# Block products for seven of u's eight column pairs, with sums made by GpSimd, and v's items ahead of them

## The chip, the cores and the metric

One core of one Trainium2 chip runs the whole kernel. The metric is the device time in microseconds of one execution; a measured time is the median over several runs. The profile shows one execution. Its engines are PE (TensorE: matmuls), PEld (TensorE's weight loads, which overlap PE), DVE (VectorE), ACT (ScalarE), POOL (GpSimd) and SP (SyncE, which here only starts DMA transfers). A profile's span runs from its first instruction to its last.

## The reference, cut to what matters

One decoder layer on x of 1024 tokens by 1024 channels, in float32. The change touches the input projection, and in it the columns of u:

```python
h = rms_norm(x, attn_norm_w[l])
proj = h @ w_in[l]
q, k, v, u, g = jnp.split(proj, splits, axis=-1)
...
u_a, u_b = jnp.split(u, 2, axis=-1)
c = causal_depthwise_conv(u_a * jax.nn.sigmoid(u_b), conv_w[l], conv_b[l])
c = jax.nn.silu(layer_norm(c, conv_ln_w[l], conv_ln_b[l]))
y_b = c @ w_proj_conv[l]
```

u has 2048 columns. Column c of its first half is multiplied with the sigmoid of column c of its second half, so the kernel works on eight column pairs: 128 columns of `u_a` and the same 128 of `u_b`. The convolution has 31 taps along the tokens and works on each channel by itself.

## The kernel before

**Numbers in two parts.** A float32 matrix is held as a high part (rounded to the matmul's type, by `split_hi` on ScalarE, line 120) and a low part (the rest, source less high part, by `split_lo` on VectorE, line 125, or by GpSimd in `wsplit`, line 284, while `low_by_pool` is set). A product of two matrices is three matmuls per block: high by high, high by low, low by high (`mm3`, lines 162 to 164).

**The first stage**, from the start to about 320 us. `opening` normalizes x, turns it and writes h transposed as `hT_hi` and `hT_lo` (128 partitions x 8 blocks of the contraction x 1024 tokens), beside v's first 256 columns and the first half of u's pair 0. Then come items in a list: `first`, which is U1, V1, U2, U3, V2, U4, Q0, V3, U5, U6, U7. A `U` item (`u_item`, `u_half`) takes a column pair: for each half of the tokens it makes the gate's product (`gemm_T`, 8 blocks x 3 matmuls of 512 tokens into one PSUM bank), the sigmoid on ScalarE, the other product, their multiplication on VectorE from PSUM (line 601), and a store to `u_d`. A `V` item makes 256 columns of v for all tokens in four yields (`gemm_N`, matmuls of 256 columns), splits them (`v_split`) and stores them; a `Q` item makes one head's q and k in four yields, normalizes them, and turns them with `turn_qk`, whose results are copied between partition halves by SP's DMAs (line 800 on).

**Weights** come through `ws`, a stream of planned loads: a DMA on SP's queue into one of two buffers `wraw`, then the split into `whi` and `wlo` of 1024 columns, of which there are three each. `ws.ahead` says how many loads are made before they are asked for.

**The convolution** is a background list, `bg`. When a pair's u is stored, `conv_load` (its reload) and 31 taps are added: a first tap (line 570, VectorE) and 30 more (line 578, VectorE), each a multiply-add of up to 1023 tokens onto a running sum. The sums of channels 0 to 3 (`CONV_PSUM`) lie in PSUM, one at a time, and are copied out by ScalarE after the last tap (line 582); those of channels 4 to 7 lie in SBUF. After every yield of the first stage `bg.step` issues on average 3.25 entries (`TAPS_FIRST`), behind the last low part made by VectorE. What is left is spread over the attention stage by its slack on VectorE, and must be done at that stage's end.

**The bias rows** (`bias_rows`, at n = 16): GpSimd's queue loads a table of one-hot rows `oh` and the bias table `rb`, TensorE multiplies them in three pieces of 384 columns, ScalarE copies the pieces into `gr`, and one DMA on GpSimd's queue stores all to `b_d`. `bias_skew(h)`, one per head, are further DMAs on GpSimd's queue, at every third yield from n = 18.

**What sets the order.** Each engine runs its instructions in one queue, in an order that is fixed when the kernel is built, by a planner that follows the order in the program and its own estimate of when an instruction is ready; `after(ins)` puts the instructions of a block behind `ins` on its engine. An instruction that waits holds everything behind it on its engine. A buffer of a tag with `bufs=n` is reused after n tiles.

**The gate/up stage** late in the kernel already uses seven products where eight are plain: `prepare(f)` makes the sums of weight quarters, `differences` makes the sums of the activations (`T`), `product` is one block product (4 blocks x 3 matmuls onto one bank), and `pair` runs the seven over three PSUM banks a, b, c. A bank that is used a second or third time keeps on accumulating, and what it holds in between is copied out.

Of the kernel before, what the change touches and what calls it, by code (L numbers as in the profile page):

```python
# [16 lines left out]
P = 128  # L17
# [40 lines left out]
def kernel(  # L58
# [48 lines left out]
    sm.tile([P, 40], F32, name="pad_sm", bufs=1)  # L107
# [19 lines left out]
    low_by_pool = [False]  # L127

# [43 lines left out]
    pg2 = a0.enter_context(tc.tile_pool(name="pg2", bufs=2, space=PSUM))  # L172
# [107 lines left out]
    def wsplit(raw, tiles=wtiles):  # L280
        hi, lo = tiles()
        split_hi(hi[:], raw[:])
        if low_by_pool[0]:
            pool.tensor_tensor(lo[:], raw[:], f32(hi[:]), op=ALU.subtract)
        else:
            split_lo(lo[:], raw[:], hi[:])
        return hi, lo
# [100 lines left out]
    first = ["U1", "V1", "U2", "U3", "V2", "U4", "Q0", "V3", "U5", "U6", "U7"]  # L388
# [11 lines left out]
    TAPS_FIRST = 3.25  # L400
# [11 lines left out]
    for it in ["U0"] + first + [x_ for l_ in later for x_ in l_]:  # L412
        ws.plan(loads_of(it))
# [148 lines left out]
    def conv_taps(c):  # L562
        acc = []

        def first_tap():
            if c < CONV_PSUM:
                acc.append(pcv[0].tile([P, S], F32, tag="acc", name=f"acc{c}", bufs=1))
            else:
                acc.append(cv.tile([P, S], F32, tag="acc", name=f"acc{c}", bufs=1))
            dve.tensor_scalar(  # L570
                acc[0][:], us[c][:], cw[:, c, CW - 1 : CW], pcol("conv_b", c), op0=ALU.mult, op1=ALU.add
            )
# [140 lines left out]

    def v_split(o, j, i2):
        vh = ap.tile([P, 512], F32R, tag="vh", name=nm("vh"))
        vl = ap.tile([P, 512], F32R, tag="vl", name=nm("vl"))
# [17 lines left out]
    def bias_rows():  # L734

        oh = ap.tile([NB + 1, TL], F32, name="oh", bufs=1)
        pool.dma_start(oh[:], buckets)
        rb = ap.tile([NB + 1, H], F32, name="rb", bufs=1)
        pool.memset(rb[:], -BIG)
        pool.dma_start(rb[:NB, :], rel_bias)  # L740
        dve.tensor_scalar(rb[:], rb[:], -1.0, None, op0=ALU.mult)
        gr = ap.tile([H, TL], F32, name="gr", bufs=1)
        for c0 in range(0, TL, 384):
            o = pm()
            pe.matmul(o[:H, :384], rb[:], oh[:, c0 : c0 + 384], start=True, stop=True)
            act.copy(gr[:, c0 : c0 + 384], o[:H, :384])
        pool.dma_start(b_d[:], gr[:])
# [87 lines left out]

    def opening():


        nonlocal qkp
# [131 lines left out]
        pcv.append(pcv_ctx.enter_context(tc.tile_pool(name="pcv", bufs=1, space=PSUM)))  # L971
        low_by_pool[0] = True
# [8 lines left out]
    for _ in chain(opening(), run(first)):  # L981
# [4 lines left out]
        if n >= 18 and n % 3 == 0 and (n - 18) // 3 < H:  # L986
            bias_skew((n - 18) // 3)
# [816 lines left out]
```

## Time and profile before

| what | us |
|---|---|
| median of 3 runs | 1760.24 (1760.22 to 1760.38) |
| the profiled execution | 1758.51 |
| its span | 1756.7 |
| TensorE busy (a model of overlapped matmuls) | 1744.9 |
| VectorE busy | 1251.9 |
| ScalarE busy | 816.9 |
| GpSimd busy | 82.0 |

A row of the costliest groups gives line, engine, operation, written and read tiles with their shapes, the count, then busy us and mean ns of one, then the idle time before them and what ended it. A row of the timeline gives start, duration, engine, line and operation, neighbours of one kind merged with their count; in brackets stands the idle time before it and what ended it. A row of a tile or a line gives the count, the smallest, median and largest duration in ns, and the first and the last start. A row of TensorE's waits gives who waited, for whom, the total in us, the times and the longest. A row of DMA issues ends with the KB of each and the us to landing.

### The profile page before, as it was taken

The numbers are of one execution on the slowest core, as the hardware profiler recorded it, in microseconds if no ns is written. First come the engines' busy times: TensorE is split into PE (matmuls) and PEld (weight loads), VectorE is DVE, ScalarE is ACT, GpSimd is POOL, SyncE is SP. The second block draws the span as 40 slices with busy tenths as digits, with TensorE's granted clock in tenths as the row PEclk, the third lists the DMA queues.
The fourth block names the chain that finished last, engine by engine and source line by source line (L and its number), as shares of the span: only waits on it lengthen the run. The fifth ranks groups of instructions, "written<-read, shape, count | busy, mean of one in ns | idle before, by whom it ended". The sixth has DMA issues, their size and how long they took to land.

```text
span 1756.7 us, 25779 instructions
## 1 busy us (share of the span) xinstructions
PE 1744.9 (99%) x9377; PEld 1503.8 (86%) x9377; DVE 1251.9 (71%) x2084; ACT 816.9 (47%) x1900; POOL 82.0 (5%) x121
## 2 busy tenths in 40 slices
PE   9999999999999999999999999999999999999999
PEld 7888998989998998988788788888888888888887
DVE  7487878798888988977778534877667666565544
ACT  5121341667677777755457313643333333333332
POOL 2113222000000000000000000000000000000000
PEclk9999999999999999999999999999999999999999
DMA  6246363143335344343873544234544544598663
GB/s 208 86 132 210 108 199 102 43 145 102 98 110 151 100 121 127 91 138 121 286 248 106 168 168 144 91 102 151 173 150 160 177 154 140 168 359 286 215 217 131
DMA packets 253156, 271.68 MB, mean 155 GB/s; under 512 B 15666, under 2 KB 177498, under 8 KB 253028
## 3 DMA queue, kind: packets, MB, share of 16 engines
q1 hardware_dynamic: 250848, 263.25, 46.3%
q0 software_dynamic: 1744, 5.19, 1.0%
q8 instruction: 74, 1.21, 0.3%
q10 hardware_dynamic: 436, 1.58, 0.3%
q14 instruction: 54, 0.44, 0.1%
HBM read 175.55 MB, written 78.16 MB: 144 GB/s over the span
## 4 chain that ended last, share of the span: by engine, by line
PE 94%; DVE 3%; DMA 1%; ACT 1%; issue 1%; SPq 0%; DVEq 0%
PE acc L1650 22%; PE pg L164 14%; PE pg L162 14%; PE pg L163 14%; PE acc L494 12%; PE sc L1043 2%; PE sc L1042 2%; PE pT L1081 2%; PE wo L164 2%; PE wo L163 2%; PE wo L162 2%; DVE acc L578 1%; PE pW L162 1%; PE pW L163 1%; PE pW L164 1%; PE pg L863 1%
## 5 line engine op out<-in xcount | busy, mean ns | idle before, releaser
L578 DVE SCALAR_TENSOR_TENSOR acc<-u,cw,acc 128x1023 f32<-128x1023 f32 (+14 forms) x240 | 307.3, 1281 | 3.8
L120 ACT CAST whi<-wraw 128x1024 fp32r<-128x1024 f32 x107 | 112.5, 1053 | 200.7 <-PE pg L163 95.3
L162 PE MATMUL pg<-hT_hi,whi 128*128 128x512 f32 x512 | 201.7, 394 | 0.0
L163 PE MATMUL pg<-hT_lo,whi 128*128 128x512 f32 x512 | 201.0, 393 | 0.0
L164 PE MATMUL pg<-hT_hi,wlo 128*128 128x512 f32 x512 | 200.8, 393 | 0.0
L162 PE MATMUL pg<-whi,hT_hi 128*128 128x256 f32 x704 | 199.6, 284 | 0.0
L164 PE MATMUL pg<-whi,hT_lo 128*128 128x256 f32 x704 | 199.6, 284 | 0.0
L163 PE MATMUL pg<-wlo,hT_hi 128*128 128x256 f32 x704 | 199.4, 283 | 0.0
L125 DVE TENSOR_TENSOR wlo<-draw,whi 128x1024 fp32r<-128x1024 f32 x75 | 91.7, 1223 | 85.8 <-ACT whi L120 77.6
L125 DVE TENSOR_TENSOR wlo<-wraw,whi 128x1024 fp32r<-128x1024 f32 x85 | 103.6, 1219 | 60.3 <-ACT whi L120 60.1
L120 ACT CAST whi<-draw 128x1024 fp32r<-128x1024 f32 x75 | 79.1, 1055 | 129.5 <-PE acc L494 116.0
L163 PEld LDWEIGHTS pg<-wlo,hT_hi 128*128 128x128 f32 x704 | 134.5, 191 | 1.8
L162 PEld LDWEIGHTS pg<-whi,hT_hi 128*128 128x128 f32 x704 | 134.3, 191 | 1.7
L164 PEld LDWEIGHTS pg<-whi,hT_lo 128*128 128x128 f32 x704 | 134.4, 191 | 1.2
L494 PE MATMUL acc<-wlo,whi 128*128 128x512 f32 x308 | 119.8, 389 | 0.0
L494 PE MATMUL acc<-whi,wlo 128*128 128x512 f32 x308 | 119.8, 389 | 0.0
L1049 ACT ACTIVATE E<-E,mn 128x640 f32<-128x640 f32 (+7 forms) x128 | 99.6, 780 | 41.3 <-DVE mn L1044 40.9
L164 PEld LDWEIGHTS pg<-hT_hi,wlo 128*128 128x128 f32 x512 | 96.2, 188 | 19.7 <-issue 0.6
L162 PEld LDWEIGHTS pg<-hT_hi,whi 128*128 128x128 f32 x512 | 96.3, 188 | 18.7 <-issue 0.6
L163 PEld LDWEIGHTS pg<-hT_lo,whi 128*128 128x128 f32 x512 | 96.3, 188 | 18.6
L1044 DVE CUSTOM_DVE_ANT_0 E<-sc,tb 128x512 f32<-128x512 f32 (+3 forms) x128 | 74.0, 585 | 31.2 <-PE pT L1081 16.1
L1650 PE MATMUL acc<-h_hi,whi 128*128 128x512 f32 x240 | 93.4, 389 | 0.0
(299 smaller groups left out, 4097.3 us busy)
## 6 DMA issues: line engine op xcount, KB each, us to landing
wraw<-in_w_gate_up_dram SPq DMA_DIRECT2D x44, 512.0 KB, 4.6
wraw<-in_w_in_dram SPq DMA_DIRECT2D x40, 512.0 KB, 4.0
qs<-qs SPq DMA_DIRECT2D x96, 128.0 KB, 2.3
wd<-in_w_down_dram SPq DMA_DIRECT2D x44, 256.0 KB, 3.2
tdT<-wd SPq DMA_DIRECT2D x88, 128.0 KB, 4.8
draw<-sdS SPq DMA_DIRECT2D x44, 256.0 KB, 3.4
draw<-tdT SPq DMA_DIRECT2D x44, 256.0 KB, 3.6
wraw<-in_w_in_dram SPq DMA_DIRECT2D x32, 256.0 KB, 3.2
```

Source lines behind the costliest of these rows:

```text
L120: act.copy(dst, src)
L125: last_lo[0] = dve.tensor_tensor(dst, src, f32(hi), op=ALU.subtract).ins
L162: pe.matmul(o, lh, rh, start=start, stop=False)
L163: pe.matmul(o, lh, rl, start=False, stop=False)
L164: last_mm[0] = pe.matmul(o, ll, rh, start=False, stop=stop).ins
L494: m = pe.matmul(o[s_][i][:], l_[:, ts], r_[:, 512:], start=start and j + y_ == 0, stop=j == n - 1 and y_ == 2, skip_group_check=not start,)
L578: dve.scalar_tensor_tensor(a_, us[c][:, : S - n], cw[:, c, t : t + 1], a_, op0=ALU.mult, op1=ALU.add)
L1042: pe.matmul(o[:, :w], qh[:, qs], k, start=True, stop=False)
L1043: last_mm[0] = pe.matmul(o[:, :w], ql[:, qs], k, start=False, stop=True).ins
L1044: dve.tensor_tensor_reduce(e[:, ks], o[:, :w], tb[:, S - nk + c0 : S - nk + c0 + w], 1.0, mn[:, j : j + 1] if c0 else 3.0e38, ALU.add, ALU ...
L1049: act.activation(e[:, :nk], e[:, :nk], AF.Exp, bias=mn[:, j : j + 1], scale=-1.0, accum_out=l[:, j : j + 1])
L1650: pe.matmul(o[:], a_[x_][:, k, :], b_[y_][:, k, :], start=start and k + x_ + y_ == 0, stop=k == 3 and x_ == 1, skip_group_check=not start,)
```

## The change

For u's pairs 1 to 7 the eight quarter products (two column blocks x two halves of the contraction x two halves of the tokens) are replaced by seven block products, each of half the contraction and half the tokens, on sums of quarters:

- `sums_of_h` makes the four sums of h's quarters, T1 to T4: GpSimd joins high and low part of each quarter (8 additions of 1024 columns), VectorE makes the differences (8 subtractions of 1024), ScalarE the high parts and GpSimd the low parts (8 of 1024). It is issued in three steps after each of the first four yields.
- `prepare` is moved out of the gate/up stage and takes its source as arguments; while `low_by_pool` is set GpSimd makes its four weight sums (512 columns each) and the low parts. In the gate/up stage it is called as before, through `prep`.
- `u_pair` runs the seven products with four yields a pair, the copies, sigmoids and sums of each output half, one multiplication on GpSimd and one on VectorE, the two stores, and adds the convolution's entries.
- `first_stage` replaces the list: V1, V2, then U1 to U7, then Q0 and V3. The weights of pair 1 are loaded at n = 4 and prepared by n = 7 of its own count.
- The first tap of a channel goes from VectorE to ScalarE; 2.75 background entries are issued for each yield, behind VectorE's last instruction, and after the first stage entries are issued until channels 0 to 3 are complete.
- `bias_rows` works in three calls (n = 18, 19, 20), each with its own load, matmul, copy and store, in buffers of the u stage; the skews come at every second yield from n = 24.
- The tiles of `opening` are released before the u stage, whose rooms `tt` and `st` take their place and that of `qkp`, which is opened after it. PSUM banks of `pg2` stay open to the end of the stage.

```diff
-    first = ["U1", "V1", "U2", "U3", "V2", "U4", "Q0", "V3", "U5", "U6", "U7"]
+    first = ["V1", "V2"]
+    last = ["Q0", "V3"]
...
-            dve.tensor_scalar(
-                acc[0][:], us[c][:], cw[:, c, CW - 1 : CW], pcol("conv_b", c), op0=ALU.mult, op1=ALU.add
-            )
+            act.activation(acc[0][:], us[c][:], AF.Identity, bias=pcol("conv_b", c), scale=cw[:, c, CW - 1 : CW])
...
+    def bias_rows(c0):
+
+        if c0 == 0:
+            pool.memset(rb[:], -BIG)
+            pool.dma_start(rb[:NB, :], rel_bias)
+            dve.tensor_scalar(rb[:], rb[:], -1.0, None, op0=ALU.mult)
+        oh, gr = half("u3")[: NB + 1, :384], half("u2")[:H, :384]
+        pool.dma_start(oh, buckets[:, c0 : c0 + 384])
+        o = pm()
+        pe.matmul(o[:H, :384], rb[:], oh, start=True, stop=True)
+        act.copy(gr, o[:H, :384])
+        pool.dma_start(b_d[:, c0 : c0 + 384], gr)
...
+        def add(j, l):
+            def go():
+                for e in range(2):
+                    ks = slice(4 * j + 2 * e, 4 * j + 2 * e + 2)
+                    pool.tensor_tensor(
+                        F[j, l][:, two[e], :], f32(hT_hi[:, ks, TOK[l]]), f32(hT_lo[:, ks, TOK[l]]), op=ALU.add
+                    )
+
+            return go
+
+        def less(o, a_, b_):
+            def go():
+                for e in two:
+                    dve.tensor_tensor(*[F[x_][:, e, :] for x_ in (o, a_, b_)], op=ALU.subtract)
+
+            return go
...
+        def parts(z, tags, src, eng):
+            def go():
+                hi, lo = [room(t_, F32R, f"T{z}{e}") for t_, e in zip(tags, "hl")]
+                v = src or fourth
+                for e, v_ in zip(two, v):
+                    split_hi(hi[:, e, :], v_)
+                for e, v_ in zip(two, v):
+                    eng.tensor_tensor(lo[:, e, :], v_, f32(hi[:, e, :]), op=ALU.subtract)
+                TS[z] = hi[:], lo[:]
+
+            return go
...
+        return [
+            add(*f11), add(*f12), less(f11, f12, f11), add(*f22), less(f12, f22, f12), less(f22, f22, f11),
+            parts(2, ("y0", "y1"), halves(f22), pool), add(*f21), parts(1, ("y2", "y3"), halves(f11), pool), less4,
+            parts(3, ("x00", "x11"), halves(f12), pool), parts(4, ("x01", "x10"), None, pool),
+        ]
...
+        s12, s34 = [s_pool.tile([P, 1024], F32, tag=t_, name=nm(t_), bufs=1) for t_ in ("s12", "s34")]
+        A["11"], A["12"] = parts(*[t_[:] for t_ in wsplit(raws[0])])
+        eng = pool if low_by_pool[0] else dve
+        eng.tensor_tensor(s12[:, 0:512], a21, a22, op=ALU.add)
+        eng.tensor_tensor(s12[:, 512:1024], s12[:, 0:512], a11, op=ALU.subtract)
+        eng.tensor_tensor(s34[:, 0:512], a11, a21, op=ALU.subtract)
+        eng.tensor_tensor(s34[:, 512:1024], a12, s12[:, 512:1024], op=ALU.subtract)
+        yield A
+        A["S1"], A["S2"] = parts(*[t_[:] for t_ in wsplit(s12)])
+        yield
+        A["S3"], A["S4"] = parts(*[t_[:] for t_ in wsplit(s34)])
+        hi, lo = [s_pool.tile([P, 512], F32R, tag=t_, name=nm(t_), bufs=s_bufs) for t_ in ("sh", "sl")]
+        split_hi(hi[:], a22)
+        low(lo[:], a22, hi[:])
...
+    def u_pair(c, A, ahead):
+
+        B = {(j, l): (hT_hi[:, KH[j], TOK[l]], hT_lo[:, KH[j], TOK[l]]) for j in range(2) for l in range(2)}
+        a, b, c_ = acc(), acc(), acc()
+        product(b, A["11"], B[0, 0], True)
+        p1 = half("p1")
+        act.copy(p1, b[:])
+        product(a, A["12"], B[1, 0], True)
+        dve.tensor_tensor(p1, a[:], p1, op=ALU.add)
+        act.activation(p1, p1, AF.Sigmoid)
+        nxt = next(ahead, None)
+        yield
+        product(b, A["S2"], TS[2], False)
+        u2 = half("u2")
+        act.copy(u2, b[:])
+        product(c_, A["S1"], TS[1], True)
+        u3 = half("u3")
+        act.copy(u3, c_[:])
+        next(ahead, None)
+        yield
+        product(b, A["S3"], TS[3], False)
+        dve.tensor_tensor(u3, b[:], u3, op=ALU.add)
+        product(c_, A["S4"], B[1, 1], False)
+        dve.tensor_tensor(u2, c_[:], u2, op=ALU.add)
+        act.activation(u2, u2, AF.Sigmoid)
+        pool.tensor_tensor(u3, u3, u2, op=ALU.mult)
+        nc.sync.dma_start(u_d[c][:, TOK[1]], u3)
+        yield
+        product(b, A["22"], TS[4], False)
+        dve.tensor_tensor(p1, b[:], p1, op=ALU.mult)
+        nc.sync.dma_start(u_d[c][:, TOK[0]], p1)
+        bg.todo.insert(max(0, len(bg.todo) - CW), conv_load(c))
+        bg.add(conv_taps(c))
+        next(ahead, None)
+        yield
+        return nxt
+
+    def first_stage():
...
+        for n, _ in enumerate(run(first)):
+            for _ in range(3):
+                if tsum:
+                    tsum.pop(0)()
+            if n == 1:
+                ws.ahead = 1
+                ws.fetch()
+                ws.ahead = 0
+            if n == 4:
+                next(ups[0])
+            if n == 5:
+                A = next(ups[0])
+            if n in (6, 7):
+                next(ups[0])
+            yield
+        for c in range(1, NKT):
+            ahead = ups[c] if c < NKT - 1 else weights_ahead()
+            next(ahead)
+            A = yield from u_pair(c, A, ahead)
...
-        if n == 16:
-            with after(last_of(mybir.EngineType.DVE)), after(bias_anchor[0]):
-                bias_rows()
-        if n >= 18 and n % 3 == 0 and (n - 18) // 3 < H:
-            bias_skew((n - 18) // 3)
-        due += TAPS_FIRST
-        with after(last_lo[0]):
+        if n in (18, 19, 20):
+            with after(bias_anchor[0]):
+                bias_rows(384 * (n - 18))
+        if n >= 24 and n % 2 == 0 and (n - 24) // 2 < H:
+            bias_skew((n - 24) // 2)
+        due += 2.75
+        with after(last_of(mybir.EngineType.DVE)):
             bg.step(int(due))
...
+    bg.until((NKT - CONV_PSUM) * (CW + 1) - 1)
     low_by_pool[0] = False
```

More of the change, by code (lines that the diff above doesn't have):

```diff
@@ L282, in wsplit @@
         split_hi(hi[:], raw[:])
[L283 to L286, printed above, removed]
+        low(lo[:], raw[:], hi[:])
         return hi, lo
```

154 lines of the change are left out of this document (89 added, 65 removed).

## The prediction

> **What bounds the kernel now.** I read the totals by engine first, then the longest waits of TensorE, then busy times by stage: 58 to 320 us is the stage of v, u and the first q/k, 320 to 830 attention, 1173 to 1560 the gate/up product, which already works in blocks.
>
> ```profile
> span 1756.7 us, 25779 instructions
> PE 1744.9 (99%) x9377; PEld 1503.8 (86%) x9377; DVE 1251.9 (71%) x2084; ACT 816.9 (47%) x1900; POOL 82.0 (5%) x121
> ...
> PE pg L162 <- DVE gt L1378: 2.9, 1, 2.9
> PE pm L200 <- DVE busy L187: 1.5, 1, 1.5
> ...
> 58.00:96.00 38.00, 38.00 (x200) 32.78 (x199) 22.07 (x20) 6.38 (x8) 7.19 (x3) 1.00 0.36 116
> 96.00:320.00 224.00, 224.00 (x1339) 198.95 (x1338) 183.30 (x171) 58.73 (x130) 51.75 (x30) 1.00 0.45 144
> 320.00:830.00 510.00, 509.55 (x3423) 467.80 (x3422) 428.75 (x963) 358.44 (x1194) 10.91 (x60) 1.00 0.38 112
> 1173.00:1560.00 387.00, 387.00 (x1709) 320.45 (x1708) 250.61 (x370) 132.78 (x181) 0.00 (x0) 1.00 0.52 167
> ```
>
> The columns of a stage are its length, then busy us (count) of PE, PEld, DVE, ACT and POOL, and the granted clock. TensorE is never idle in the stage that changes, and its clock is 1.00, so a matmul taken away there shortens the kernel unless another engine turns late. VectorE is busy 205 of the 262 us there, GpSimd 59.
>
> **The saving.** Matmuls overlap, so a busy duration is not what one costs. The spacing of starts is:
>
> ```profile
> 284.80 0.39 PE L162 MATMUL pg<-hT_hi,whi 128*128 128x512 f32 x1
> ...
> 303.83 0.39 PE L162 MATMUL pg<-hT_hi,whi 128*128 128x512 f32 x1
> ...
> L1669 ACT COPY u<-acc x20: 567/587/587, 1173.0 to 1532.5; 128x512 f32<-128x512 f32 x20
> ```
>
> Between the first two rows lie 28 rounds of three, 84 matmuls: 19.03 us, 0.2266 each. A u pair is now 2 matrices x 2 halves of the tokens x 8 blocks x 3 terms = 96 matmuls, 21.75 us. Seven products of 4 blocks x 3 terms are 84, 19.03 us. The gate/up stage runs just this form: its copy at L1669 comes once a pair, and 20 of them span 359.5 us, 18.92 us a pair, no stall left in it. Over seven pairs, 84 matmuls go: 84 x 0.2266 = **-19.0 us**. (By the 0.39 us of a row it would be 33; that counts overlapped time.)
>
> **GpSimd's new work.** Per pair it gets three low parts of 1024 columns, and four sums, one low part and one product of 512.
>
> ```profile
> L284 POOL TENSOR_TENSOR wlo<-wraw,whi 128x1024 fp32r<-128x1024 f32 x22 | 54.0, 2461 | 215.0 <-ACT whi L120 200.7 <-DVE acc L578 13.9 <-DMA u<-u_d 0.4
> L284 POOL TENSOR_TENSOR wlo<-wraw,whi x22: 2379/2400/3389, 67.6 to 311.1; 128x1024 fp32r<-128x1024 f32 x22
> L125 DVE TENSOR_TENSOR wlo<-wraw,whi 128x1024 fp32r<-128x1024 f32 x85 | 103.6, 1219 | 60.3 <-ACT whi L120 60.1
> L1678 DVE TENSOR_TENSOR u<-acc,u x20: 681/691/692, 1180.8 to 1540.2; 128x512 f32<-128x512 f32 x20
> L1071 POOL MEMSET ph<- 128x128 f32 x32 | 6.6, 205 | 0.2 <-ACT ar L1095 0.2
> ```
>
> 1024 columns take 2.40 us. No GpSimd sum of 512 is in the trace: at least 1.20 (half), at most 2.40. A 128-column fill takes only 0.2, so little of 2.40 is fixed; VectorE's ratio of 512 to 1024 is 0.691/1.219 = 0.57, and I take 1.35. That is 3 x 2.40 + 6 x 1.35 = 15.3 us a pair (14.4 to 21.6) under 19.0 of TensorE: hidden, with 3.7 us to spare.
>
> **VectorE and the shared reads.** Does GpSimd's load slow the convolution taps?
>
> ```profile
> 136.56 13.07 DVE L578 SCALAR_TENSOR_TENSOR acc<-u,cw,acc 128x1016 f32<-128x1016 f32 x10
> ...
> 137.90 2.41 POOL L284 TENSOR_TENSOR wlo<-wraw,whi 128x1024 fp32r<-128x1024 f32 x1
> ...
> 294.78 2.77 POOL L284 TENSOR_TENSOR wlo<-wraw,whi 128x1024 fp32r<-128x1024 f32 x1 [3.05 <-ACT whi L120]
> 311.10 3.39 POOL L284 TENSOR_TENSOR wlo<-wraw,whi 128x1024 fp32r<-128x1024 f32 x1 [13.55 <-ACT whi L120]
> ...
> 295.89 2.75 DVE acc L578
> 312.28 3.30 DVE acc L578
> ```
>
> Ten taps of channel 1, whose sum lies in PSUM, run at 1.31 us each straight through a GpSimd operation. A tap of channel 4, whose sum lies in SBUF, takes 2.75 or 3.30 us when it meets one, and both end together. In the new u stage every VectorE operation (taps of channels 0 to 3, the sums on a product) has a PSUM operand; only the eight 1024-column subtractions of `sums_of_h` have two SBUF inputs. [...]
>
> A pair gives VectorE four yields x 2.75 taps = 11 x 1.31 plus 4 x 0.69 = 17.2 us of 19.0. Its tightest point: the sum on the third use of bank b must be done while the S4 product runs (12 x 0.2266 = 2.7 us). It costs nothing while the queue keeps its 1.8 us of slack. At three channel changes the old first tap gives way to two ScalarE operations in a row:
>
> ```profile
> L582 ACT COPY done<-acc 128x1024 f32<-128x1024 f32 x4 | 4.0, 1010 | 0.5 <-DVE acc L578 0.5
> 72.89 1.35 DVE L570 TENSOR_SCALAR acc<-u,cw,pvec 128x1024 f32<-128x1024 f32 x1 [5.40 <-DMA u<-u_d]
> ```
>
> Copy and first tap are 1.01 + about 1.05, less the 1.35 saved: the taps come 0.7 us later, inside the slack. Channel 1 starts from an empty list, and its first tap now waits in ScalarE's queue for the load (5.4 us here), ahead of copies that must be done within 2.7 us. Zero if those are queued first, 5.4 - 2.7 = 2.7 if not; with the changes I take **+1** (0 to 4).
>
> **The seam from v to u.** V1 and V2 now cover the sums of h.
>
> ```profile
> 66.80 0.69 DVE L601 TENSOR_TENSOR sg<-pg,sg 128x512 f32<-128x512 f32 x1 [3.42 <-PE pg L164]
> 94.86 0.69 DVE L125 TENSOR_TENSOR vl<-pg,vh 128x512 fp32r<-128x512 f32 x1 [2.57 <-ACT vh L120]
> 100.62 0.69 DVE L125 TENSOR_TENSOR vl<-pg,vh 128x512 fp32r<-128x512 f32 x1
> 56.66 0.36 SPq L720 DMA_DIRECT2D v_lo<-vl  x1
> ```
>
> U0 ends at 66.8 and a yield of v takes 5.76 us, so eight end at 112.9, and the third product, the first with a low part of sums, is due 24 matmuls later, 118.3. GpSimd cannot start before the buffers of V0's last store (56.66 plus some 3) are free: 60, or 67 if it is held to V1. Before that product stand 16 operations of 2.40 (38.4), V2's two low parts (4.8), and U1's first: 2.40 + 4 x 1.35 + 2.40 = 10.2. That is 53.4: done at 113 to 120. Each subtraction that takes the reads adds up to 1.22: 8 x 1.22 = 9.8, so 113 to 130, a stall of 0 to 12; I take **+3**, as V2's second half must also wait for V1's weights to come free.
>
> **The bias rows** move from one block to three, at n = 18 to 20, in buffers of the u stage, through GpSimd's queue.
>
> ```profile
> 128.93 0.54 POOL L747 DMA_DIRECT2D b_d<-gr  x1 [12.93 <-ACT gr L746]
> 131.42 3.58 POOL L750 DMA_DIRECT2D t_d<-b_d  x7 [1.95 <-DMA b_d<-gr]
> 135.00 2.41 POOL L284 TENSOR_TENSOR wlo<-wraw,whi 128x1024 fp32r<-128x1024 f32 x1
> ...
> 130.26 1.05 ACT L120 CAST whi<-wraw 128x1024 fp32r<-128x1024 f32 x1 [1.62 <-PE pg L163]
> ```
>
> GpSimd stood 12.93 us at the store of the bias rows for ScalarE's copy, and the low part whose high part was ready at 131.3 started only at 135.0, behind seven issues. In U1 and U2, lows and sums would stand behind such a store. Three waits of 0 to 12.9 against 2 x 3.7 of slack: 0 to 31 us. Where the old store waited, no arithmetic stood ready behind it, so I take a few us each, mostly in the slack: **+3**.
>
> **Attention.** Taps left for it:
>
> ```profile
> L578 DVE SCALAR_TENSOR_TENSOR acc<-u,cw,acc x135: 1179/1273/3285, 74.3 to 318.2; 128x1023 f32<-128x1023 f32 x5, 128x1022 f32<-128x1022 f32 x5, 128x1021 f32<-128x1021 f32 x5, 128x1020 f32<-128x1020 f32 x5
> L578 DVE SCALAR_TENSOR_TENSOR acc<-u,cw,acc 128x1008 f32<-128x1008 f32 (+14 forms) x105 | 132.2, 1259 | 0.1
> ```
>
> 105 now; after, four whole channels, 120. Fifteen more x 1.26 = 19 us put VectorE at 448 of 510 us, still under TensorE. The last six taps and the copy (6 x 1.31 + 1.01 = 8.9 us) fall just before attention, whose score banks wait for that sum; fill matmuls can run meanwhile. Zero to 9, I take **+1**.
>
> **What only moves.** V1 and V2 go ahead of U1, Q0 and V3 behind U7.
>
> ```profile
> wraw<-in_w_in_dram SPq DMA_DIRECT2D x40, 512.0 KB, 4.0
> qs<-qs SPq DMA_DIRECT2D x96, 128.0 KB, 2.3
> ```
>
> Q0's turned halves are copied through SP's queue, 2.3 us each; three u items used to lie between them and attention, now only V3, 4 x 5.76 = 23 us. The second half's eight copies (six of q, two of k) take 8 x 2.3 = 18 us at most, one after another, so V3 hides them; without it the first scores would wait up to those 18. The weights of a pair are the same two 512 KB loads, 4.0 us each, asked for one pair (19 us) ahead. One store of u now waits on SP's queue for GpSimd's product instead of VectorE's, and the loads behind it with it; 19 us of lead cover that at any price above. The eight skew issues, 3.58/7 = 0.51 us each, come every second yield (9.5 us) on GpSimd's queue: 4.1 us out of 7 x 3.7 of slack, nothing.
>
> Sum: the profiled execution took 1758.5 us (span 1756.7). 1758.5 - 19.0 + 1 + 3 + 3 + 1 = 1747.5. The shown median is 1.7 above that execution: **1749** us.
>
> **Rivals.**
> - All of it hidden: 1760.2 - 19.0 = 1741. For: the gate/up stage's 18.92 us. Against: there GpSimd does nothing and VectorE is busy 251 of 387 us, 65%, not 17.2 of 19.0, 90%.
> - GpSimd becomes the bound of a pair: at 2.40 for 512 columns too it needs 21.6 us, 7 x 2.6 = 18 given back: 1759. Against: the 0.2 us fill.
> - Slower: GpSimd's queue stands at the three bias stores as it did at the one. 3 x 12.93 - 7.4 of slack = 31.4 us of stall in U1 and U2: 1760.2 - 19.0 + 31.4 = 1773. It decides from 26.4 us of waiting, 8.8 a store. For: the 12.93. Against: then nothing else was ready, so the wait hurt nobody and need not recur.
> - The engines exclude each other: 17.2 + 15.3 = 32.5 us a pair, 7 x 13.5 = 94 more: 1835. The ten taps at 1.31 us speak against it.
>
> That the change doesn't remove what it says can hardly be: the matmuls are written out, and PE's count must fall by 84.
>
> **The numbers.** The forecast 0.58 (its own range 1743 to 1756), all hidden 0.18, GpSimd-bound 0.09, slower by the queue 0.14, exclusion 0.01. A measurement of this kernel can't tell less than 0.2%, 3.5 us, from no change. Faster: 0.58 + 0.18 + a third of 0.09 = 0.79; same: half of that case, 0.04; slower: the rest, 0.17. Range 1741 to 1760: it takes in the unknown costs up to 19 us and leaves out the two slower rivals.
>
> **What would show it.** PE's count at 9293; U1 to U7 about 19 to 20 us apart by the first copy of each pair, more in U1 and U2 than later; GpSimd near 15 us a pair, its 512-column sums at 1.35; taps at 1.3 in the u stage; PE waits on GpSimd at U1's third product of a few us; 120 taps after the stage. It is wrong if pairs stay near 21 us (GpSimd or VectorE the bound), if one wait of over 10 us stands at U1 or U2, or if attention grows by more than 3 us.

## The result and the profile after

Median 1769.28 us over nine runs (1763.56 to 1772.34), against 1759.63 (1758.26 to 1762.02) for the kernel before on the same chip: a ratio of **1.0050, 95% interval 1.0037 to 1.0063**. The change makes the kernel 0.5% slower. The forecast was 1749, in a range of 1741 to 1760.

The page of the kernel after, its first lines:

```profile
span 1765.4 us, 25829 instructions
PE 1735.8 (98%) x9293; PEld 1493.0 (85%) x9293; DVE 1267.4 (72%) x2098; ACT 856.5 (49%) x1952; POOL 198.7 (11%) x190
```

The 84 matmuls are gone (9377 to 9293), and the span is 8.7 us longer. The product that closes a half of a pair on GpSimd (line 981) comes once a pair; in GpSimd's timeline of the kernel after, in pairs 4 and 7:

```profile
210.84 1.29 POOL L981 TENSOR_TENSOR u<-u,u 128x512 f32<-128x512 f32 x1
...
268.09 1.30 POOL L981 TENSOR_TENSOR u<-u,u 128x512 f32<-128x512 f32 x1
```

57.25 us for three pairs, 19.1 each: in its steady part the stage does what was forecast. So the time was lost in other places. TensorE's five longest waits of the kernel after between 85 and 360 us (who waited for whom; us in total, times, longest):

```profile
PE acc L944 <- ACT whi L120: 4.0, 1, 4.0
PE pg L168 <- DVE u L125: 3.7, 2, 2.3
PE sc L1243 <- ACT done L584: 3.0, 1, 3.0
PE pg L168 <- ACT whi L120: 1.5, 1, 1.5
PE pg L169 <- POOL wlo L131: 0.7, 1, 0.7
```

Each is short, and their sum is 12.9. The kernel before shows one wait here, of 0.5 us. The windows of the kernel after show what comes on top (length, busy of PE, PEld, DVE, ACT, POOL, granted clock, DMA share, GB/s):

```profile
90.00:100.00 10.00, 6.19 (x33) 5.61 (x32) 9.93 (x9) 4.37 (x5) 10.00 (x5) 0.70 0.28 95
...
160.00:170.00 10.00, 9.75 (x43) 7.73 (x42) 9.25 (x10) 3.28 (x5) 9.99 (x10) 1.00 1.02 317
170.00:180.00 10.00, 6.40 (x29) 4.96 (x27) 8.71 (x7) 1.25 (x2) 1.08 (x1) 0.97 0.95 295
180.00:190.00 10.00, 9.56 (x30) 7.67 (x31) 3.58 (x4) 3.07 (x6) 8.86 (x7) 0.69 0.28 87
...
330.00:340.00 10.00, 6.96 (x34) 6.24 (x33) 5.07 (x16) 8.31 (x23) 0.00 (x0) 0.66 0.28 106
```

In three windows the granted clock falls to about 0.7. The trace's clock records have half speed from 94.06, 179.39 and 332.99 us on, 6.83 us each time; the kernel before has none between 58 and 860 us. A stretch of matmuls at half speed looks busy in a window (9.56 us with 30 matmuls in 180 to 190, 9.75 with 43 in 160 to 170), so I counted in another way: for each matmul the time to the next one's start, less the median of that for its number of columns, summed over a stretch. That is what TensorE lost there, by idling or by a slow clock (us, one profiled execution each, so differences of 1 or 2 us between two kernels are not to be read closely):

| stretch | before | after | what lies there in the kernel after |
|---|---|---|---|
| 0 to 85 | 10.3 | 10.3 | opening |
| 85 to 120 | 0.0 | 8.3 | V1 to V2 |
| 120 to 160 | 1.5 | 1.9 | U1, U2, bias rows |
| 160 to 195 | 0.0 | 7.6 | U3, U4 |
| 195 to 300 | -0.1 | -0.1 | U5 to U7, Q0 |
| 300 to 360 | 0.8 | 6.9 | V3, start of attention |
| 360 to 600 | 0.7 | 0.6 | attention |
| 600 to 900 | 7.6 | 11.7 | end of attention and behind it |
| rest | 0.9 | 1.9 | |
| sum | 21.8 | 49.2 | |

27.4 more lost, 19.0 saved: +8.4, against +8.7 in the span. Of the three new losses (8.3, 7.6 and 6.1, 22 us), 12.9 are waits; the rest is for the most part the slow clock behind them.

**First place, 85 to 120.** VectorE's timeline in the kernel after (start, duration, line, operation; `u<-pg,p` of line 125 is here v's low part, in a room of the u stage):

```profile
72.11 9.53 DVE L873 TENSOR_TENSOR F<-F,F 128x1024 f32<-128x1024 f32 x3
81.57 0.68 DVE L125 TENSOR_TENSOR u<-pg,p 128x512 fp32r<-128x512 f32 x1
82.17 2.82 DVE L873 TENSOR_TENSOR F<-F,F 128x1024 f32<-128x1024 f32 x1
...
88.25 3.42 DVE L880 TENSOR_TENSOR T<-F,F 128x1024 f32<-128x1024 f32 x1
91.60 1.27 DVE L580 SCALAR_TENSOR_TENSOR acc<-u,cw,acc 128x1022 f32<-128x1022 f32 x1
92.79 0.68 DVE L125 TENSOR_TENSOR u<-pg,p 128x512 fp32r<-128x512 f32 x1
```

and TensorE's there:

```profile
90.95 0.28 PE L170 MATMUL pg<-whi,hT_lo 128*128 128x256 f32 x1
93.52 0.38 PE L168 MATMUL pg<-whi,hT_hi 128*128 128x256 f32 x1 [2.29 <-DVE u L125]
...
94.55 0.41 PE L168 MATMUL pg<-whi,hT_hi 128*128 128x256 f32 x1
94.77 0.41 PE L169 MATMUL pg<-wlo,hT_hi 128*128 128x256 f32 x1
```

GpSimd's timeline in the kernel after shows what reads beside the subtractions:

```profile
60.05 23.86 POOL L864 TENSOR_TENSOR F<-hT_hi,hT_lo 128x1024 f32<-128x1024 f32 x8 [37.09 <-DMA v_lo<-vl]
...
87.21 6.68 POOL L890 TENSOR_TENSOR T1l<-F,T1h 128x1024 fp32r<-128x1024 f32 x2
```

A subtraction takes 1.6 to 3.4 us while GpSimd reads at the same time, and 1.21 where nothing of GpSimd's runs beside it (only the chain on VectorE, below). v's low part, which frees a PSUM bank, stands behind one of 3.42 us and a tap. TensorE waits 2.29 us, and then its matmuls of 256 columns are 0.21 us apart instead of 0.12: half speed. Two more waits follow: 1.5 us for the high part of V2's weights, which stands in ScalarE's queue behind the high parts of T3, and 1.4 for v's low part.

**Second place, 160 to 195.** GpSimd's timeline in the kernel after:

```profile
158.38 4.12 POOL L756 DMA_DIRECT2D t_d<-b_d  x8 [0.41 <-issue]
162.51 1.31 POOL L929 TENSOR_TENSOR s<-wraw,s 128x512 f32<-128x512 f32 x1
```

and the chain that ended last, in order of time (start, us, what):

```profile
162.00 0.51 POOL t_d L756
...
162.51 1.32 POOL s L929
...
163.84 15.47 DMA wraw<-in_w_in_dram
...
179.34 1.05 ACT whi L120
...
180.44 11.61 PE acc L944 x38
```

The program asks for one skew at every second yield, but all eight are issued in one block, ahead of a weight sum that frees the load buffer. The load of U4's weights starts at 163.84, into 4.7 MB of skews (8 x 576 KB; DMA share 0.95 to 1.02), and takes 15.47 us instead of 4.

**Third place, the start of attention.** ScalarE's timeline in the kernel after:

```profile
328.62 1.28 ACT L630 ACT_TABLE_LOAD   x1
329.91 0.22 ACT L630 ACTIVATE t<-v 128x16 f32<-128x16 f32 x1
330.15 1.28 ACT L631 ACT_TABLE_LOAD   x1
331.44 0.21 ACT L631 ACTIVATE r<-t 128x16 f32<-128x16 f32 x1
331.56 0.57 ACT L777 COPY qkraw<-pg 128x512 f32<-128x512 f32 x1
333.06 1.01 ACT L584 COPY done<-acc 128x1024 f32<-128x1024 f32 x1 [0.93 <-DVE acc L580]
```

Lines 630 and 631 are the two steps of one inverse square root, a logarithm and an exponential; a table load of 1.28 us stands before each. VectorE's timeline, and the first scores in TensorE's:

```profile
331.69 0.17 DVE L635 TENSOR_TENSOR t<-r 128x16 f32<-128x16 f32 x1 [1.72 <-ACT r L631]
331.78 1.25 DVE L580 SCALAR_TENSOR_TENSOR acc<-u,cw,acc 128x994 f32<-128x994 f32 x1
...
334.13 0.80 PE L1243 MATMUL sc<-ks,qs 128*128 128x512 f32 x1 [3.04 <-ACT done L584]
```

Channel 3's last tap on VectorE (331.78 to 333.03) stands behind line 635, which waited for the exponential. The copy of its sum (line 584) frees the PSUM bank of the first scores.

### The profile page after: what moved, and what is told of

Same layout as the page of the kernel before. It is cut to its first block, busy times and chain, and to the rows that moved or that the text cites. A ratio compares the mean times of both kernels' runs of the same rounds, so it can differ in the third digit from the quotient of the medians.

```text
span 1765.4 us, 25829 instructions
## 1 busy us (share of the span) xinstructions
PE 1735.8 (98%) x9293; PEld 1493.0 (85%) x9293; DVE 1267.4 (72%) x2098; ACT 856.5 (49%) x1952; POOL 198.7 (11%) x190
## 4 chain that ended last, share of the span: by engine, by line
PE 88%; DVE 4%; ACT 2%; DMA 2%; POOL 2%; issue 1%; SPq 0%; ACTq 0%; DVEq 0%; POOLq 0%
PE acc L944 29%; PE acc L498 12%; PE pg L168 10%; PE pg L169 10%; PE pg L170 10%; PE sc L1243 2%; PE sc L1244 2%; PE pT L1282 2%; PE wo L168 2%; PE wo L170 2%; PE wo L169 2%; POOL F L864 1%; PE pW L169 1%; PE pW L168 1%; PE pW L170 1%
## 5 line engine op out<-in xcount | busy, mean ns | idle before, releaser
L120 ACT CAST whi<-wraw 128x1024 fp32r<-128x1024 f32 x100 | 105.0, 1051 | 125.9 <-PE wo L170 48.1
L168 PE MATMUL pg<-hT_hi,whi 128*128 128x512 f32 x288 | 114.2, 396 | 0.0
L169 PE MATMUL pg<-hT_lo,whi 128*128 128x512 f32 x288 | 114.1, 396 | 0.0
L170 PE MATMUL pg<-hT_hi,wlo 128*128 128x512 f32 x288 | 113.6, 394 | 0.0
L120 ACT CAST whi<-s 128x1024 fp32r<-128x1024 f32 x54 | 56.8, 1052 | 98.5 <-PE acc L944 83.0
L944 PE MATMUL acc<-h_lo,whi 128*128 128x512 f32 x240 | 93.4, 389 | 0.0
L944 PE MATMUL acc<-h_hi,wlo 128*128 128x512 f32 x240 | 90.1, 389 | 0.0
```

What stands on the lines that cost most here:

```text
L120: act.copy(dst, src)
L168: pe.matmul(o, lh, rh, start=start, stop=False)
L169: pe.matmul(o, lh, rl, start=False, stop=False)
L170: last_mm[0] = pe.matmul(o, ll, rh, start=False, stop=stop).ins
L944: last_mm[0] = pe.matmul(o[:], a_[x_][:, k, :], b_[y_][:, k, :], start=start and k + x_ + y_ == 0, stop=k == 3 and x_ == 1, skip_group_che ...
```

## The experiments

Theory: the loss is these three places, and each goes when its own cause is taken away. Rivals: the waits move on to the next place; or the order of the items itself is what costs.

**The skews one by one.** The kernel after, with

```diff
-            bias_skew((n - 24) // 2)
+            with after(last_of(mybir.EngineType.Pool)):
+                bias_skew((n - 24) // 2)
```

> Edit: each of the eight skew issues keeps its place in GpSimd's queue, behind the GpSimd instruction in front of it in the program, in place of all eight together. Theory (the burst of 4.7 MB makes one weight load of pair U4 take 15.5 us, TensorE waits 4.2 us and then runs a half-clock window): the 7.6 us lost between 160 and 195 us go, 1769.3 becomes about 1762. Rival (the load is late because GpSimd frees its buffer late, the burst is chance): the load still starts late and TensorE still waits 3 us or more there, 1767 to 1769. Rival (GpSimd's load bounds every pair): no change.

1766.87 us (1765.82 to 1768.67), 1.0031 (1.0018 to 1.0044) of the kernel before. The block of eight is gone (one or two per pair from 186 us on), and so is the loss at 160 to 195: 1.9 instead of 7.6. But this execution lost 3.0 at 195 to 300 and 4.6 at 360 to 600, where the kernel after lost nothing and 0.6. The time missed the theory's 1762, and its interval and that of the kernel after (1.0037 to 1.0063) overlap: the place is shown, a gain in time is not. (The weight loads of 512 KB between 130 and 260 us took 5.1 us in the median now, which bears out that the burst made the one of 15.47.)

**More taps late in the stage.**

```diff
-        due += 2.75
+        due += 2.75 if n < 44 else 3.75
```

> Edit: from the 44th yield on (Q0 and V3) 3.75 background entries a yield in place of 2.75, so that no taps are left to force at the end of the stage. Theory (the first scores wait for the bank of channel 3's sum, 3.2 us, and that starts a half-clock window): the 5.9 us lost between 322 and 360 us go, about 1763.5. Rival (the wait at the first scores is for the turned halves of k, since only V3 now covers them): the wait stays with another releaser, 1767 to 1769.

1771.23 (1766.60 to 1772.41), 1.0053 (1.0038 to 1.0068): no gain. The first scores still waited, now 3.1 us for VectorE's sums of scores and bias (line 1245). The theory missed; the wait stayed with another releaser, as the rival had it, but not for the halves of k.

**The additions on VectorE**, the subtractions as they were:

```diff
-                    pool.tensor_tensor(
+                    dve.tensor_tensor(
```

> Edit: the eight additions of high and low part of h on VectorE in place of GpSimd. Theory (VectorE's eight subtractions are blocked by GpSimd's additions, take 23 us in place of 10, and v's low parts behind them hold the PSUM banks): additions 8 x 1.22 = 10 us from about 58 us, subtractions near 1.22 each, the waits between 85 and 120 us and their half-clock window go, 8.3 us, about 1761. Rival (VectorE has simply too much to do beside the taps in V1 and V2): more work on it makes the waits of TensorE for v's low parts longer, 1770 or more. Rival (GpSimd late at U1): GpSimd ends some 19 us earlier; nothing changes if TensorE did not wait for it.

1768.00 (1767.34 to 1769.94), 1.0042 (1.0027 to 1.0057). This lies between the theory's 1761 and the rival's 1770, and the interval overlaps with that of the kernel after. The loss at 85 to 120 fell from 8.3 to 3.6, with no slow clock: one wait of 2.4 for v's low part stayed, and the 1.2 left over is less than the 1.7 that the shortest stretch of half speed seen, 3.41 us, would add. Why none followed this wait, when one followed the wait of 2.29 in the kernel after, is not shown. Ahead of v's low parts four subtractions still took 10.66 us and the next two 6.38, now beside GpSimd's low parts.

**The order alone**: the kernel before with V1, V2, U1 to U7, Q0, V3 as its list.

> Edit: the kernel before, with its item list in the new order (V1, V2, U1 to U7, Q0, V3) and nothing else. Theory (the order alone costs little, as its stalls come from the sums): TensorE's waits at V1 to V2 under 1 us, some 7 taps more in attention, 1759.6 becomes 1760 to 1763. Rival (the order itself is what starves the taps and crowds attention's start): 1766 or more.

1764.75 (1763.26 to 1766.54), 1.0020 (1.0010 to 1.0029). The move that was priced at nothing costs 3.4 us by the medians (1761.33 before), more than the theory's 1760 to 1763 and less than the rival's 1766. In the kernel with only the order changed, VectorE's timeline and the wait are:

```profile
314.97 0.81 DVE L570 TENSOR_SCALAR acc<-u,cw,pvec 128x1024 f32<-128x1024 f32 x1 [3.76 <-DMA c_d<-done]
315.82 4.62 DVE L578 SCALAR_TENSOR_TENSOR acc<-u,cw,acc 128x1023 f32<-128x1023 f32 x2
320.36 0.69 DVE L125 TENSOR_TENSOR vl<-pg,vh 128x512 fp32r<-128x512 f32 x1
```

```profile
PE pg L162 <- DVE vl L125: 2.8, 1, 2.8
```

V3's low part stood behind a channel's first tap, which had waited 3.76 us for a store of the finished sum, and behind a tap with its sum in SBUF, which met GpSimd (two taps in 4.62 us, not 2.54). TensorE waited 2.8, and half speed followed from 322.64 on (granted clock 0.83 in 322 to 332).

**More taps all along.**

```diff
-        due += 2.75
+        due += 3.25
```

> Taps at 3.25 a step instead of 2.75; everything else as in the changed kernel. Theory (what was lost at the attention's start and end, about 6 + 3 us, is background work left over): fewer taps are forced out before the first scores and about 117 instead of 120 are left, the first scores no longer wait 3.0 us, and the time falls by 4 to 9 us, to 1760-1765. Rival (VectorE has no room beside the u pairs: 13 taps of 1.31 and 2.8 of sums make 19.8 us against 19.0 of TensorE): the sums of the block products come late, waits of TensorE appear between 195 and 300 us, where there are none now, and the time stays at 1765-1773.

1763.73 (1761.20 to 1767.06), 1.0019 (1.0010 to 1.0029): 5.5 us less than after, inside the theory's range and clear of the interval of the kernel after. The loss at 300 to 360 fell from 6.9 to 2.0, at 600 to 900 from 11.7 to 7.4, and u's pairs lost 0.7 at 195 to 300. 3.0 came up at 360 to 600.

**Additions on VectorE, subtractions on GpSimd**, alone and with two edits from above (skews one by one, taps at 3.25):

```diff
-                    pool.tensor_tensor(
+                    dve.tensor_tensor(
...
-                    dve.tensor_tensor(*[F[x_][:, e, :] for x_ in (o, a_, b_)], op=ALU.subtract)
+                    pool.tensor_tensor(*[F[x_][:, e, :] for x_ in (o, a_, b_)], op=ALU.subtract)
...
-                dve.tensor_tensor(d[:], F[f21][:, e, :], F[f22][:, e, :], op=ALU.subtract)
+                pool.tensor_tensor(d[:], F[f21][:, e, :], F[f22][:, e, :], op=ALU.subtract)
```

> [...] Theory (the 8.3 us lost at 85-120 are v's low parts behind the blocked subtractions, and the half-clock window that the wait opens): no wait of TensorE for u's low part above 1 us there, no half-clock stretch, the loss at 85-120 under 2 us, the total 6 to 8 us less, 1761-1763. Rival (any GpSimd chain of this length is late): GpSimd then has some 53 us from about 65 us on, done at about 118, and TensorE waits for the sums at U1's products instead, 3 to 10 us at 118-140, and the total stays within 3 us of 1769.

> Three edits together: skews one by one in GpSimd's order, taps at 3.25, additions on VectorE with subtractions on GpSimd. Theory (the three places lost 8.3, 7.6 and 6 us, and nothing else is wrong with the change): 1769 - 17 to 22, so 1747 to 1752, faster than the kernel before by 0.5%. Rival (each removed wait is followed by the next one in the same queue): 1756 to 1765.

> The changed kernel unaltered, beside the three others on one chip. Theory and rival alike: 1764 to 1772; where its half-clock stretches lie in this execution shows whether they follow the three waits (94, 179 and 333 us) or come at random.

The swap took 1775.98 (1773.85 to 1777.46), the three edits together 1766.80 (1761.45 to 1769.52), and the kernel after, unaltered beside them, 1769.57 (1768.53 to 1773.12). The swap and the three edits lie outside the ranges of theory and rival both. In the swap the loss at 85 to 120 fell to 1.0, but the wait had moved ahead of it. VectorE's timeline in the swapped kernel:

```profile
60.34 17.87 DVE L864 TENSOR_TENSOR F<-hT_hi,hT_lo 128x1024 f32<-128x1024 f32 x8 [2.02 <-DMA v_hi<-vh]
78.13 3.36 DVE L125 TENSOR_TENSOR wlo<-wraw,whi 128x1024 fp32r<-128x1024 f32 x1
```

Eight additions in a block, stretched to 17.87 us beside GpSimd's subtractions (9.17 without them, with only the chain on VectorE, below), stand ahead of the low part of V1's weights: TensorE waits 9.6 us for it. To split the chain differently between the two engines leaves the conflict in it. The unaltered kernel has half speed at 96.5, 181.9 and 338.9 us, near its three places again (granted clock 0.83 in 90 to 100, 0.66 in 180 to 190, 0.77 in 340 to 345); at 600 to 900 it lost 15.2 this time.

**The whole chain on GpSimd**, with skews one by one and taps at 3.25 or 3.5; and those two edits without it:

> Three edits: the eight subtractions on GpSimd too (the additions stay there), skews one by one in GpSimd's order, taps at 3.25. Theory (v's low parts are held up only by VectorE's subtractions, which wait for GpSimd's turn at their shared inputs; VectorE has no work in the chain now): no wait of TensorE for DVE u or DVE wlo at 55-120, loss there under 2 us instead of 8.3; with 4 to 6 us won by the taps and 5 by the skews, 1750 to 1757, faster than the kernel before. Rival (24 instructions of 2.40 us make 58 us of GpSimd, too late for U1): TensorE waits on POOL's parts at 118-140 for 3 to 8 us, and the time is 1757 to 1765.

> As the run before it, with taps at 3.5 a step instead of 3.25. Theory (background work left over is what the attention still pays for): 1 to 3 us less than with 3.25. Rival (VectorE is full beside the u pairs: 14 taps of 1.31 and 2.8 are 21.1 us against 19.0): waits of TensorE for VectorE's sums or for PSUM at 195-300, 2 to 8 us more.

> Skews one by one and taps at 3.25, subtractions left on VectorE. Theory: the loss of 8 us at 85-120 stays and the other two fall, so 1757 to 1763, and 6 to 8 us above the run with the subtractions on GpSimd. Rival (the 85-120 wait is another queue's, ScalarE's or the DMA's): no more than 2 us between the two.

1769.01 (1768.00 to 1774.93), 1774.05 (1773.26 to 1774.99) and 1762.70 (1761.47 to 1766.18). The theory missed. The waits were those of the rival, GpSimd's queue, but some came earlier than it had them, and the time lies above its 1757 to 1765. Taps at 3.5 were 5.0 us slower than at 3.25 by the medians, as that run's rival had it. And the kernel with the subtractions left on VectorE was 6.3 us faster than the one with the chain on GpSimd, where I had expected it to be slower. TensorE's waits between 85 and 145 us, with the chain on GpSimd and taps at 3.25,

```profile
PE acc L944 <- ACT whi L120: 7.1, 2, 6.7
PE pg L169 <- POOL wlo L131: 4.4, 1, 4.4
```

The first is U1's weights, whose sums on GpSimd began at 127.0 instead of 115.4 us; the second is the low parts of V2's weights, made at 98.6 to 103.2 in the middle of the chain.

The last of these three runs differs from the one with taps at 3.25 by the skews alone: 1.0018 of the kernel before against 1.0019. Its loss at 160 to 195 is 1.5 instead of 6.0, but 4.9 came up at 195 to 300, where the other lost 0.7. For the skews the rival held for the most part: what is won at their place is lost behind it.

**The whole chain on VectorE** (additions, subtractions, and the low parts of T1 to T4), and the stores of the bias rows issued by ScalarE:

```diff
-                    pool.tensor_tensor(
+                    dve.tensor_tensor(
...
-                    eng.tensor_tensor(lo[:, e, :], v_, f32(hi[:, e, :]), op=ALU.subtract)
+                    dve.tensor_tensor(lo[:, e, :], v_, f32(hi[:, e, :]), op=ALU.subtract)
...
-        pool.dma_start(b_d[:, c0 : c0 + 384], gr)
+        nc.scalar.dma_start(b_d[:, c0 : c0 + 384], gr)
```

With skews one by one and taps at 3.25: first the chain alone, then the stores with only the additions on VectorE, then all.

> All 24 instructions of the chain of h's sums on VectorE (additions, subtractions and low parts, about 1.15 us each, 28 us), so that GpSimd and VectorE do not share inputs there; skews one by one, taps at 3.25. Theory (it is the sharing that stretches, not the work): no VectorE instruction of the chain longer than 2 us, no wait above 1 us and no half-clock stretch at 85-120, loss there under 2 us, and 1753 to 1758. Rival (VectorE's queue has no 28 us to give beside v's low parts): v's low parts are still late and the time is 1760 to 1766, as with the subtractions alone.

> Only the additions on VectorE; skews one by one; taps at 3.25; and the three stores of the bias rows issued by ScalarE, so that GpSimd's queue does not wait for TensorE's bias products. Theory (GpSimd's idle 4 to 5 us at 141 is what makes the weights of the next pairs late): GpSimd has no such idle time at 140-160, TensorE no wait for ACT whi at 160-200, and the losses of 160-195 and 195-300 together stay under 2 us instead of 6 to 8; 1754 to 1760. Rival (the weights are late by their buffers and loads, not by GpSimd): the wait of 2.5 us near 195 stays, 1758 to 1763.

> The two together: the whole chain on VectorE and the bias rows' stores issued by ScalarE, skews one by one, taps at 3.25. Theory: 1748 to 1755, under the kernel before. Rival: no better than the better of the two.

| | us | ratio to before |
|---|---|---|
| chain on VectorE | 1757.08 (1751.80 to 1760.60) | 0.9982 (0.9969 to 0.9994) |
| additions on VectorE, stores by ScalarE | 1756.37 (1752.66 to 1762.07) | 0.9982 (0.9971 to 0.9994) |
| chain and stores | 1755.30 (1749.53 to 1759.03) | **0.9971 (0.9958 to 0.9984)** |

The loss at 85 to 120 is 0.6 with the chain on VectorE, and 9.7 in the same kernel with it shared (the skews and taps alone, above): the medians differ by 5.6 us, and the intervals (1.0008 to 1.0027 with it shared) lie apart. This is the theory's range, though single instructions of the chain can still meet GpSimd's (with only the chain moved, below, one subtraction took 2.83 us). The last kernel lies just above its theory's 1755. The three intervals in the table overlap, so the runs don't show that the stores gain anything. The second kernel still lost 4.0 at 85 to 120 and is no slower for it: behind it, at 120 to 160, it lost 1.8, and the first one 4.6. The idle time of GpSimd at the bias rows did not go with the stores (5.7 us up to 137.4, where the next load of the table waits for the bias product too). So that theory is not borne out, though its range of the time was met, and the losses at 160 to 300 are 5.7 instead of 6.3 with skews and taps alone.

Two more, one with only the chain moved, one with all edits and taps at 3.5:

> Only one edit to the changed kernel: all 24 instructions of the chain of h's sums on VectorE. Theory (shared inputs stretch the chain, and that costs 8 us at the seam): loss at 85-120 under 2 us with no half-clock stretch there, those at 160-195 and 322-360 stay at 5 to 8 us each, and the time is 1760 to 1763, about the kernel before's. Rival (waits removed here come back in the next place): 1765 to 1769.

> All four edits (chain on VectorE, skews one by one, bias rows' stores issued by ScalarE), taps at 3.5 a step instead of 3.25. Theory (VectorE has 19.0 us a pair, and 14 taps of 1.31 and 2.8 of sums are 21.1): taps crowd the sums, waits of TensorE at 195-300, 1 to 4 us slower than with 3.25, 1756 to 1759. Rival (the attention still pays for what is left over): 1 to 3 us faster, 1752 to 1754.

Chain only: 1765.87 (1763.48 to 1767.80), 1.0031 (1.0019 to 1.0042), 3.4 less than after where I expected 6 to 9. That is the rival's range, and the interval overlaps with that of the kernel after. VectorE's timeline in it:

```profile
59.82 9.17 DVE L864 TENSOR_TENSOR F<-hT_hi,hT_lo 128x1024 f32<-128x1024 f32 x8 [1.76 <-DMA v_hi<-vh]
68.91 1.22 DVE L125 TENSOR_TENSOR wlo<-wraw,whi 128x1024 fp32r<-128x1024 f32 x1
...
87.17 0.69 DVE L125 TENSOR_TENSOR u<-pg,p 128x512 fp32r<-128x512 f32 x1
...
91.23 0.69 DVE L125 TENSOR_TENSOR u<-pg,p 128x512 fp32r<-128x512 f32 x1
```

The additions take 1.15 us each and the low parts come in time; the loss at 85 to 120 is 0.0. Those at 160 to 195 and 300 to 360 stay as they were, 8.2 and 7.2; 120 to 160 lost 1.3 more and 600 to 900 3.6 more; the granted clock was 0.993 in this execution, 0.991 in the second one of the kernel after. So the place was right, and part of its gain was given back behind it, as the rival had it. Taps at 3.5: 1757.35 (1755.09 to 1761.13), 0.9986 (0.9977 to 0.9995), which the intervals do not tell from 3.25; 7.8 lost at 360 to 600, where 3.25 loses 0.7.

## Why the prediction failed, by its steps

The sum had 8 us of new losses against 19.0 saved; 27.4 came. The saving and GpSimd's work were right. The seam from v to u, the start of attention and what "only moves" were not.

- **The saving** held: 84 matmuls less, 19.1 us a pair, and by the loss table 27.4 lost less 8.7 in the span, so 18.7 saved.
- **GpSimd's new work** held. In the groups of the kernel after the sums of 512 columns take 1.29 (taken as 1.35), so a pair is 3 x 2.40 + 6 x 1.30 = 15.0 us, and the stage from U5 on lost nothing:

```profile
L926 POOL TENSOR_TENSOR s<-wraw 128x512 f32<-128x512 f32 x7 | 9.0, 1289 | 8.8 <-DMA wraw<-in_w_in_dram 8.8
```

- **VectorE and the shared reads** (+1): taps with a sum in PSUM ran at 1.27 us beside GpSimd, as forecast, and U5 to U7 lost nothing. But one reading is wrong: the slow taps and GpSimd's operations do not end together. In the rows shown there GpSimd ends at 297.55 and 314.49, and the taps end 1.1 us later, at 298.64 and 315.58. A tap of 1.29 us was held up by 1.5 and 2.0, GpSimd's 2.40 by 0.4 and 1.0: most of the delay fell on VectorE, and those rows showed it.
- **The seam from v to u** (+3): the step that failed first. The prediction saw that the eight subtractions would meet GpSimd and put 1.22 us on each, but counted them on GpSimd's side alone, against U1's third product. GpSimd's timeline and TensorE's in the kernel after:

```profile
121.40 4.77 POOL L131 TENSOR_TENSOR wlo<-s,whi 128x1024 fp32r<-128x1024 f32 x2 [0.84 <-ACT whi L120]
...
126.47 0.39 PE L944 MATMUL acc<-T1h,whi 128*128 128x512 f32 x1
```

What the prediction had counted, down to U1's first low part of a sum, was done near 123.8, inside its 113 to 130 and after the 118.3 at which it had the product. TensorE did not wait there only because it came 8.2 us late itself, at 126.47. The cost came ahead of that, through the other engine. The stretched subtractions stood in VectorE's queue ahead of v's low parts, and those hold PSUM banks that TensorE waited for, 2.29 and 1.4 us. Measured: 8.3, and 0.0 with the chain on VectorE. That 8.3 lies inside the term's 0 to 12 is luck: the wait that was priced did not occur.
- **The bias rows** (+3, up to 31): 0.4 more lost at 120 to 160. With the chain on VectorE, TensorE came there earlier, and the stretch lost 1.7 to 3.1 more than in the kernel before, near the +3, though no run shows how much of it the bias rows make. The rival of slower had GpSimd's queue at the stores; its sign came true, its mechanism didn't.
- **Attention** (+1, 0 to 9): 6.1 at its start and 5.0 behind it. The wait for the last tap's bank is the one that the prediction named; its size was wrong, as fill matmuls did not cover it, and the prediction's own sign of being wrong, attention grown by more than 3 us, came up. "Still under TensorE" was right for the mean (VectorE busy 443 of 510 us) and wrong for the start. At the start, taps for channels 0 to 3 were still to do when the q/k chain had the queues; with 3.25 a step the loss there was 2.0. How much of the end is due to the 15 taps stays open: the same kernel lost 11.7 and 15.2 there in two executions; 7.4 with 3.25.
- **What only moves** (0): two failures. The skews were priced as issues on GpSimd's queue "every second yield"; they were issued in one block, and their price was their 4.7 MB, in which a weight load became 15.47 us: 7.6 lost there, though issued one by one they moved much of that loss to 195 to 300. And Q0 and V3 at the end cost 3.4 us in the kernel before: the prediction looked at the copies of q and k alone and not at V3's low parts in VectorE's queue, behind the taps.
- **The prices of stalls.** Every term was a wait. The waits came to 12.9 in the three places, the losses to 22: a pause of 2 to 4 us was followed by a stretch of half speed, which no term had.

The version with the lowest median, all four edits, loses 38.0 us by the measure of the table, 16.2 more than before, and saves the 19.0: 2.8 net, 3.2 in its span, 4.9 by the medians. It still loses 4.2 at 120 to 160, of which the kernel before loses 1.5 too, and 3.3 at 160 to 195. TensorE's waits there are 1.0 for ScalarE's copy of a bias row (line 752) and 0.7 for VectorE's product (line 985), then 1.6 and 1.2 for a low and a high part of a pair's weights. What makes these late no run tests, and how much of the order's 3.4 is among the rest stays open.

## What to carry to other kernels

When work is given to another engine, look at the queues of both engines that share its inputs: what stands behind a stretched instruction, and which bank or buffer does it hold? Here it paid to keep a chain on VectorE alone, though that was the busier engine; all on GpSimd, it came too late. Price a moved transfer by its bytes and by what else is loading at that time, with all issues of a kind in one block, and a late matmul by its wait plus the slow clock behind it (here 12.9 us of waits, 22 lost). And when a wait goes, look for what comes next in time: several of the losses taken away here came back in part behind their place.

## What the runs showed of the hardware

- **Half speed behind short waits.** Stretches at half clock lasted 6.83 us each in the kernel after and 3.41 in the kernel before (from 865.08 on; the last stretch of a run aside). In the second execution of the kernel after, one lasted about 10.2 by the granted clock, 0.83 in 90 to 100 and again in 100 to 120. In the kernel after one followed a wait of 2.29 us: the wait ended at 93.52, and half speed began at 94.06.
- **Waits of one length cost differently from run to run.** The wait for `gt` of 2.9 us is in both kernels (TensorE's timelines, before and after):

```profile
864.98 0.73 PE L162 MATMUL pg<-aTh,whi 128*128 128x512 f32 x1 [2.90 <-DVE gt L1378]
...
873.94 0.50 PE L168 MATMUL pg<-aTh,whi 128*128 128x512 f32 x1 [2.90 <-DVE gt L1579]
```

Before, half speed followed it from 865.08 on, for 3.41 us; after, none did (granted clock 1.00 from 340 to 1700). What decides this is not shown. So a loss in one execution holds a part that the same wait need not bring in another. The spread of the runs, 9 us after and 4 before, goes with the granted clock: 0.996 in the fastest of the nine runs after (1763.56), 0.990 in the slowest (1772.34).
- **An addition on GpSimd and a subtraction on VectorE, each with two inputs in SBUF, stretch each other:** from 2.40 up to 3.41 us on GpSimd, and from 1.21 (alone on VectorE) up to 3.43. Beside several such VectorE instructions in a row, a low part on GpSimd took 6.96 us (additions on VectorE, at 67.76). What this cost was decided by what stood behind: v's low part, for which TensorE waited 2.29 us.
